# Rotary embedding on one core: the two early rows of batch 0 in one transfer or in two

## The chip, the cores and the metric

The kernel runs on one core of a Trainium2 chip. The metric is the device time of one execution in microseconds (us), the median of several runs. A profile is one further execution, recorded instruction by instruction and, for the DMA engines, packet by packet. VectorE does the arithmetic, ScalarE converts types, GpSimd and SyncE issue the transfers, and 16 DMA engines carry them out. TensorE is not used.

## The reference

```python
batch, seq_len, num_heads, head_dim = (8, 2048, 16, 64)      # x is float32
x1, x2 = x[..., :32], x[..., 32:]
cos, sin = cos[None, :, None, :], sin[None, :, None, :]      # each (2048, 32)
out1 = x1 * cos - x2 * sin
out2 = x1 * sin + x2 * cos
return np.concatenate([out1, out2], axis=-1).astype(np.float32)
```

Every element of x is read once and every element of the output written once, 67.1 MB each way. The tables are the same for all batches and heads.

## The kernel before, in words

Each batch is laid over 128 partitions: partition p holds the J = 16 consecutive sequence positions 16p to 16p+15, which the texts call rows. A row has 16 heads of 64 elements, that is 1,024 elements. So one batch is a tile of 128 partitions by 16 rows by 1,024 elements. In memory a row of one partition is 4 KB of float32, a whole partition's part of a batch 64 KB.

The tile `buf` (f16) has room for five batches, and batch b lies in place b mod 5. The transfers that GpSimd issues convert on the way: a load reads float32 and writes f16 (`load`, line 71), a store reads f16 and writes float32 (`store`, line 81). All of these are tied by hand into one order, the ring (`in_ring`), which is also the order in which GpSimd issues them. They go through one queue, q0 in the profile. A load into a place that is in use waits until the store from there is done.

`rotate(b, j0, j1)` does the arithmetic on rows j0 to j1 of batch b with three VectorE operations: the swapped halves times sin into `v` (line 92), the batch times cos in place (line 98), and the sum in place (line 100). The minus sign is in the sin table, which ScalarE prepares (lines 104 and 105) as it narrows cos (line 106).

Batch 0 is treated apart, so that VectorE can begin before its big load is in. Its first two rows (JA = 2) are not loaded by GpSimd but by SyncE, as float32, into the tile `head` (line 42, queue q1, behind the sin table on the same queue). ScalarE narrows them into `buf` (line 107), VectorE rotates them, and GpSimd stores row 0 alone. The other fourteen rows come with `load(0)`. The issue order after the tables is: `load(0)`, `load(1)`; rotate rows 0 and 1 of batch 0; store row 0; load batches 2 and 3 together, and 4; rotate rows 2 to 15; store rows 1 to 15; then batch 1, batch 2 and so on. At the end the last two rows of batch 7 go out through `head` and SyncE (lines 134 and 135) behind the part of the store that the code calls `gate`.

Of the kernel before, what the change touches and what calls it, by code (L numbers as in the profile page):

```python
# [1 line left out]

# [4 lines left out]


@with_exitstack  # L10
def kernel(
    ctx: ExitStack,
    tc: tile.TileContext,
    x: bass.AP,
    cos: bass.AP,
    sin: bass.AP,
    out: bass.AP,
):
    nc = tc.nc
    f16 = mybir.dt.float16  # L20
    f32 = mybir.dt.float32

    B, S, H, D = x.shape
    Dh = D // 2
    P = nc.NUM_PARTITIONS
    J = S // P
    NBUF = 5

    const_pool = ctx.enter_context(tc.tile_pool(name="rope_const", bufs=1))
    io_pool = ctx.enter_context(tc.tile_pool(name="rope_io", bufs=1))  # L30
    tmp_pool = ctx.enter_context(tc.tile_pool(name="rope_tmp", bufs=1))

    JA = 2
    head = const_pool.tile([P, JA, H, D], f32)
    x0 = x[0].rearrange("(p j) h d -> p j (h d)", j=J)
    sin_f = const_pool.tile([P, J, Dh], f32)
    cos_f = const_pool.tile([P, J, Dh], f32)
    cos_h = const_pool.tile([P, J, Dh], f16)
    sin_h = const_pool.tile([P, J, D], f16)
    nc.scalar.dma_start(out=cos_f, in_=cos.rearrange("(p j) d -> p j d", j=J))  # L40
    nc.sync.dma_start(out=sin_f, in_=sin.rearrange("(p j) d -> p j d", j=J))
    nc.sync.dma_start(
        out=head.rearrange("p j h d -> p (j h d)"),
        in_=x0[:, 0:JA, :].rearrange("p j f -> p (j f)"),
    )

    buf = io_pool.tile([P, NBUF, J, H, D], f16)

    ring = []

    def in_ring(dma):
        if ring:
            tc.add_manual_dep(
                dma.ins,
                ring[-1].ins.name,
                mybir.DependencyInfo(mybir.DependencyClass.NoSync, mybir.DependencyReason.DATA),
                reason="order of the ring",
            )
        ring.append(dma)
        return dma  # L60

    def load(b, n=1):
        k = b % NBUF
        if n == 1:
            j0 = JA if b == 0 else 0
            dst = buf[:, k, j0:J, :, :].rearrange("p j h d -> p (j h d)")
            src = x[b].rearrange("(p j) h d -> p j (h d)", j=J)[:, j0:J, :].rearrange("p j f -> p (j f)")
        else:
            dst = buf[:, k : k + n, :, :, :].rearrange("p b j h d -> p b (j h d)")
            src = x[b : b + n].rearrange("b (p j) h d -> p b (j h d)", j=J)  # L70
        in_ring(nc.gpsimd.dma_start(out=dst, in_=src))  # L71

    def store(b, n=1, j0=0, j1=J):
        k = b % NBUF
        if n == 1:
            src = buf[:, k, j0:j1, :, :].rearrange("p j h d -> p (j h d)")
            dst = out[b].rearrange("(p j) h d -> p j (h d)", j=J)[:, j0:j1, :].rearrange("p j f -> p (j f)")
        else:
            src = buf[:, k : k + n, :, :, :].rearrange("p b j h d -> p b (j h d)")
            dst = out[b : b + n].rearrange("b (p j) h d -> p b (j h d)", j=J)  # L80
        return in_ring(nc.gpsimd.dma_start(out=dst, in_=src))  # L81

    def rotate(b, j0=0, j1=J):
        v = tmp_pool.tile([P, J, H, D], f16)
        n = j1 - j0
        js = slice(j0, j1)
        xt = buf[:, b % NBUF, js, :, :]
        shape = [P, n, H, 2, Dh]
        sin_b = sin_h[:, js, :].rearrange("p j (e d) -> p j e d", e=2).unsqueeze(2).to_broadcast(shape)
        cos_b = cos_h[:, js, :].unsqueeze(2).to_broadcast([P, n, 2 * H, Dh])  # L90
        xe = xt.rearrange("p j h (e d) -> p j h e d", e=2)
        nc.vector.tensor_mul(  # L92
            out=v[:, js, :, :].rearrange("p j h (e d) -> p j h e d", e=2),
            in0=xe[:, :, :, ::-1, :],
            in1=sin_b,
        )
        xw = xt.rearrange("p j h (e d) -> p j (h e) d", d=Dh)
        nc.vector.tensor_mul(out=xw, in0=xw, in1=cos_b)  # L98
        xa = xt.rearrange("p j h d -> p (j h d)")
        nc.vector.tensor_add(out=xa, in0=xa, in1=v[:, js, :, :].rearrange("p j h d -> p (j h d)"))  # L100

    load(0)
    load(1)
    nc.scalar.copy(out=sin_h[:, :, Dh:D], in_=sin_f)  # L104
    nc.scalar.mul(out=sin_h[:, :, 0:Dh], in_=sin_f, mul=-1.0)  # L105
    nc.scalar.copy(out=cos_h, in_=cos_f)  # L106
    nc.scalar.copy(  # L107
        out=buf[:, 0, 0:JA, :, :].rearrange("p j h d -> p (j h d)"),
        in_=head.rearrange("p j h d -> p (j h d)"),
    )  # L110
    rotate(0, 0, JA)
    store(0, 1, 0, 1)
    load(2, 2)
    load(4)
    rotate(0, JA, J)
    store(0, 1, 1, J)
    rotate(1)
    store(1)
    rotate(2)
    store(2)  # L120
    load(5, 2)
    load(7)
    rotate(3)
    rotate(4)
    store(3, 2)
    rotate(5)
    rotate(6)
    store(5, 2)
    rotate(7)
    gate = store(7, 1, 0, 9)  # L130
    store(7, 1, 9, J - JA)
    last = buf[:, 7 % NBUF, J - JA : J, :, :].rearrange("p j h d -> p (j h d)")
    dst = out[B - 1].rearrange("(p j) h d -> p j (h d)", j=J)[:, J - JA : J, :].rearrange("p j f -> p (j f)")
    nc.scalar.copy(out=head.rearrange("p j h d -> p (j h d)"), in_=last)  # L134
    end = nc.sync.dma_start(out=dst, in_=head.rearrange("p j h d -> p (j h d)"))
    tc.add_manual_dep(
        end.ins,
        gate.ins.name,
        mybir.DependencyInfo(mybir.DependencyClass.Sync, mybir.DependencyReason.DATA),
        reason="the last rows go out behind this part",  # L140
    )


# [1 line left out]
_INS = ['x', 'cos', 'sin']  # L145
_OUTS = [((8, 2048, 16, 64), 'float32')]


# [23 lines left out]
```

## Time and profile before

| what | us |
| --- | --- |
| median of three runs (316.48 to 316.59) | 316.5 |
| the profiled execution | 316.39 |
| its span, first to last instruction | 314.6 |
| VectorE busy | 209.1 |
| GpSimd busy | 8.6 |
| ScalarE busy | 6.7 |
| wait of VectorE for batch 2 to be loaded, from 72.99 us | 10.1 |
| wait of VectorE for batch 5 to be loaded, from 161.66 us | 36.1 |

The span is what the profile covers; the device time has some 1.8 us around it. The DMA queues carried 2,528 packets (99.09 MB, 98.1% of the engines' time) on GpSimd's q0, 432 packets (2.36 MB) on SyncE's q1 and 144 (0.26 MB) on ScalarE's q10. These megabytes count what was written; HBM was read for 67.63 MB and written for 67.11 MB. Of one transfer, each of the 16 engines carries the packets of eight partitions, one packet per partition, and then a 4-byte packet that closes it.

In the views, a line like "23.87 7.63 DVE L92 ..." of the timeline gives the start, the duration, the engine and the line of the kernel; what stands in brackets is how long the engine sat idle before and what released it. "POOL" is GpSimd, "SP" SyncE, "ACT" ScalarE and "DVE" VectorE, and a "q" behind a name is that engine's own queue of commands.

### The profile page before, as it was taken

The numbers are of one execution on the slowest core, as the hardware profiler recorded it, in microseconds if no ns is written. First come the engines' busy times: TensorE is split into PE (matmuls) and PEld (weight loads), VectorE is DVE, ScalarE is ACT, GpSimd is POOL, SyncE is SP. The second block draws the span as 40 slices with busy tenths as digits, with TensorE's granted clock in tenths as the row PEclk, the third lists the DMA queues.
The fourth block names the chain that finished last, engine by engine and source line by source line (L and its number), as shares of the span: only waits on it lengthen the run. The fifth ranks groups of instructions, "written<-read, shape, count | busy, mean of one in ns | idle before, by whom it ended". The sixth has DMA issues, their size and how long they took to land.

```text
span 314.6 us, 114 instructions
## 1 busy us (share of the span) xinstructions
DVE 209.1 (66%) x27; ACT 6.7 (2%) x6; POOL 8.6 (3%) x18
## 2 busy tenths in 40 slices
DVE  0039999992499999999950000899999999910000
ACT  3200000000000000000000000000000000020000
POOL 1020000000000000000010000000000000010000
DMA  7999999999999899999999999999999999999998
GB/s 240 252 242 200 200 267 200 200 267 200 200 200 325 375 500 400 400 400 533 400 200 221 246 200 200 246 221 333 400 508 425 400 400 525 408 400 400 433 425 342
DMA packets 3104, 101.71 MB, mean 323 GB/s; under 512 B 288, under 2 KB 288, under 8 KB 672
## 3 DMA queue, kind: packets, MB, share of 16 engines
q0 software_dynamic: 2528, 99.09, 98.1%
q1 hardware_dynamic: 432, 2.36, 1.9%
q10 hardware_dynamic: 144, 0.26, 0.2%
HBM read 67.63 MB, written 67.11 MB: 428 GB/s over the span
## 4 chain that ended last, share of the span: by engine, by line
DVE 65%; another core or an unknown queue 15%; DMA 7%; ACT 1%; issue 0%; DVEq 0%; ACTq 0%; PEldq 0%
DVE buf L98 22%; DVE v L92 22%; DVE buf L100 22%; DMA buf<-in_x_dram 7%; ACT head L134 1%; DVEq L92 0%; ACTq L134 0%; PEldq L167 0%
## 5 line engine op out<-in xcount | busy, mean ns | idle before, releaser
L92 DVE TENSOR_TENSOR v<-buf,sin_h 128x16384 f16<-128x16384 f16 (+2 forms) x9 | 69.7, 7744 | 66.6 <-DMA buf<-in_x_dram 51.3
L98 DVE TENSOR_TENSOR buf<-buf,cos_h 128x16384 f16<-128x16384 f16 (+2 forms) x9 | 69.7, 7744 | 0.3
L100 DVE TENSOR_TENSOR buf<-buf,v 128x16384 f16<-128x16384 f16 (+2 forms) x9 | 69.7, 7744 | 0.3
L81 POOL DMA_DIRECT2D out_dram<-buf x8 | 4.7, 584 | 219.2 <-DVE buf L100 219.2
L134 ACT CAST head<-buf 128x2048 f32<-128x2048 f16 x1 | 1.9, 1897 | 261.3 <-DVE buf L100 261.3
L71 POOL DMA_DIRECT2D buf<-in_x_dram x6 | 3.7, 628 | 49.7 <-DMA out_dram<-buf 48.9
L107 ACT CAST buf<-head 128x2048 f16<-128x2048 f32 x1 | 1.9, 1897 | 7.1 <-DMA head<-in_x_dram 7.1
L104 ACT ACT_TABLE_LOAD x1 | 1.3, 1283 | 1.2 <-PEq L156 1.2
L104 ACT CAST sin_h<-sin_f 128x512 f16<-128x512 f32 x1 | 0.6, 617 | 2.0 <-DMA sin_f<-in_sin_dram 2.0
L105 ACT ACTIVATE sin_h<-sin_f 128x512 f16<-128x512 f32 x1 | 0.6, 624 | 0.0
L106 ACT CAST cos_h<-cos_f 128x512 f16<-128x512 f32 x1 | 0.6, 601 | 0.0
L156 POOL MEMSET const-float32-0.0<- 128x1 f32 x1 | 0.1, 98 | 0.2 <-issue 0.2
L156 POOL MEMSET const-bfloat16-1.0<- 128x1 bf16 x1 | 0.1, 101 | 0.0
L156 POOL MEMSET const-uint8-127<- 128x1 uint8 x1 | 0.1, 99 | 0.0
L156 POOL MEMSET const-float32-1.0<- 128x1 f32 x1 | 0.1, 98 | 0.0
## 6 DMA issues: line engine op xcount, KB each, us to landing
buf<-in_x_dram POOLq DMA_DIRECT2D x2, 8192.0 KB, 60.3
buf<-in_x_dram POOLq DMA_DIRECT2D x3, 4096.0 KB, 57.4
out_dram<-buf POOLq DMA_DIRECT2D x1, 7680.0 KB, 73.5
out_dram<-buf POOLq DMA_DIRECT2D x1, 4608.0 KB, 28.6
buf<-in_x_dram POOLq DMA_DIRECT2D x1, 3584.0 KB, 22.5
out_dram<-buf POOLq DMA_DIRECT2D x1, 2560.0 KB, 34.1
head<-in_x_dram SPq DMA_DIRECT2D x1, 1024.0 KB, 12.0
out_dram<-head SPq DMA_DIRECT2D x1, 1024.0 KB, 8.4
```

The source lines that it names most:

```text
L71: in_ring(nc.gpsimd.dma_start(out=dst, in_=src))
L81: return in_ring(nc.gpsimd.dma_start(out=dst, in_=src))
L92: nc.vector.tensor_mul(out=v[:, js, :, :].rearrange("p j h (e d) -> p j h e d", e=2), in0=xe[:, :, :, ::-1, :], in1=sin_b,)
L98: nc.vector.tensor_mul(out=xw, in0=xw, in1=cos_b)
L100: nc.vector.tensor_add(out=xa, in0=xa, in1=v[:, js, :, :].rearrange("p j h d -> p (j h d)"))
L104: nc.scalar.copy(out=sin_h[:, :, Dh:D], in_=sin_f)
L105: nc.scalar.mul(out=sin_h[:, :, 0:Dh], in_=sin_f, mul=-1.0)
L106: nc.scalar.copy(out=cos_h, in_=cos_f)
L107: nc.scalar.copy(out=buf[:, 0, 0:JA, :, :].rearrange("p j h d -> p (j h d)"), in_=head.rearrange("p j h d -> p (j h d)"),)
L134: nc.scalar.copy(out=head.rearrange("p j h d -> p (j h d)"), in_=last)
L156: nc = _bacc.Bacc("TRN2", target_bir_lowering=False, num_devices=1)
```

## The change

SyncE asks for the two rows of `head` in two transfers, of one row each, 4 KB per partition instead of 8. Narrowing is a small function of one row, `narrow(j)`. Row 0 is narrowed and rotated early and stored as before; row 1 is narrowed after the loads of batches 2 to 4 are written down in the program, and is rotated together with rows 2 to 15. The stores, the loads and their order stay as they are, and so does the end of the kernel.

```diff
-    nc.sync.dma_start(
-        out=head.rearrange("p j h d -> p (j h d)"),
-        in_=x0[:, 0:JA, :].rearrange("p j f -> p (j f)"),
-    )
+    for j in range(JA):
+        nc.sync.dma_start(out=head[:, j, :, :].rearrange("p h d -> p (h d)"), in_=x0[:, j, :])
...
+    def narrow(j):
+        nc.scalar.copy(
+            out=buf[:, 0, j, :, :].rearrange("p h d -> p (h d)"),
+            in_=head[:, j, :, :].rearrange("p h d -> p (h d)"),
+        )
...
-    nc.scalar.copy(
-        out=buf[:, 0, 0:JA, :, :].rearrange("p j h d -> p (j h d)"),
-        in_=head.rearrange("p j h d -> p (j h d)"),
-    )
-    rotate(0, 0, JA)
+    narrow(0)
+    rotate(0, 0, 1)
     store(0, 1, 0, 1)
     load(2, 2)
     load(4)
-    rotate(0, JA, J)
+    narrow(1)
+    rotate(0, 1, J)
     store(0, 1, 1, J)
```

## Prediction

> **What bounds the kernel now.** I read the page first, its second part before its fourth, because the two disagree. The rows of slices (40 slices of 7.9 us each):
>
> ```profile
> DVE  0039999992499999999950000899999999910000
> ...
> DMA  7999999999999899999999999999999999999998
> ...
> DVE 65%; another core or an unknown queue 15%; DMA 7%; ACT 1%; issue 0%; DVEq 0%; ACTq 0%; PEldq 0%
> ```
>
> The chain gives 65% to VectorE, but VectorE has stretches of zeros and the DMA engines have none. To decide between them I cut the span at the borders of the transfer stages (busy time by stretch; the last two columns are the DMA share, 1.00 for all 16 engines busy, and GB/s written):
>
> ```profile
> 0.00:4.00 4.00, 0.00 (x0) 1.28 (x1) 1.41 (x6) 1.00 0.53 169
> 4.00:24.00 20.00, 3.80 (x4) 3.55 (x4) 1.80 (x3) 1.00 1.08 255
> 24.00:45.00 21.00, 20.93 (x3) 0.00 (x0) 0.00 (x0) 1.00 1.01 225
> 45.00:102.00 57.00, 46.67 (x7) 0.00 (x0) 1.08 (x2) 1.00 1.01 226
> 102.00:159.00 57.00, 56.80 (x7) 0.00 (x0) 1.24 (x2) 1.00 1.02 427
> 159.00:217.00 58.00, 21.75 (x4) 0.00 (x0) 1.27 (x2) 1.00 1.01 226
> ```
>
> From 4 us on the share is 1.00 or more, whatever VectorE does: 56.80 of 57 us in one stretch, 21.75 of 58 in another. (Loads show half the GB/s because they write 2 bytes for 4 read; above 1.00, because packet records overlap by some 0.02 us.) I added up from the packet records how many of the 16 engines had a packet open at each moment: they lose 1.86 us before 2 us of the span, 0.24 us from 2 to 4, 0.21 us after 312, and nothing worth counting between. The span is therefore the time that 16 busy engines need for a fixed set of packets, and the chain's 65% is work beside them. The start, where the change lies:
>
> ```profile
> 1.17 0.43 SPq L42 DMA_DIRECT2D head<-in_x_dram  x1
> 1.24 1.21 POOL L71 DMA_DIRECT2D buf<-in_x_dram  x2 [0.80 <-PEq L167]
> ...
> 5.51 0.60 ACT L106 CAST cos_h<-cos_f 128x512 f16<-128x512 f32 x1
> 13.22 1.90 ACT L107 CAST buf<-head 128x2048 f16<-128x2048 f32 x1 [7.11 <-DMA head<-in_x_dram]
> 15.15 1.23 DVE L92 TENSOR_TENSOR v<-buf,sin_h 128x2048 f16<-128x2048 f16 x1 [15.15 <-ACT buf L107]
> ...
> 19.19 0.54 POOL L81 DMA_DIRECT2D out_dram<-buf  x1 [16.74 <-DVE buf L100]
> 19.72 1.27 POOL L71 DMA_DIRECT2D buf<-in_x_dram  x2
> 23.87 7.63 DVE L92 TENSOR_TENSOR v<-buf,sin_h 128x14336 f16<-128x14336 f16 x1 [4.98 <-DMA buf<-in_x_dram]
> ```
>
> The head's 8 KB packets (eight per engine, 0.309 us each) run alone from 3.65 us. At 5.49 us the GpSimd queue q0 gets its first packet, 2.13 us long, and from there each engine takes one packet of q0 and one of SyncE's q1 in turn. Most engines have passed six head packets by then; the other two and the closing 4-byte packet each wait for one of q0's, so the head is in at 12.93 and ScalarE starts 0.29 us later.
>
> **The change part by part.**
>
> *The split transfer.* Per engine, eight 8 KB packets and one closing packet become sixteen of 4 KB and two closing ones. A 4 KB packet on q1 isn't in the trace. Its neighbours there are 2 KB at one packet each 0.080 us and 8 KB at one each 0.306 us; the straight line gives 0.155 us, so 16 × 0.155 = 2.48 us for 8 × 0.306 = 2.45: +0.03 us. One closing packet more: +0.01 to 0.02 us. A q1 packet that alternates with q0's shows 0.322 us for 0.309, and some three more will alternate: 3 × 0.013 = +0.04 us. At the end SyncE waits for one more semaphore, 0.06 us a step in its row of waits, partly behind the last landing: 0 to 0.06 us. Ends: as lower end 0 (the same bytes; a gain from a fuller start could not exceed the 0.24 us lost from 2 to 4 us), as upper end the 4096-byte packets of the early store, at least 0.172 us each, so 16 × 0.172 − 2.45 = +0.30 us. I take the line, because it joins rows of the same queue and direction: +0.1 us in all.
>
> *Is the second transfer there in time?* SyncE's first issue at 0.74 has its first packet at 1.74, 1.00 us later; the head's issue at 1.17 is followed by packets at 3.65, directly behind the sin table's. The second row's issue would run from about 1.6 to 2.0 us. Row 0 takes 8 × 0.155 = 1.24 us, from 3.65 or 3.88 by engine, up to 4.9 or 5.13. ScalarE's cos transfer, issued in the same moment as sin's, has its first packet 0.77 us behind sin's; as spacing between two transfers this puts row 1's packets at 3.65 + 0.77 = 4.42 at the latest, 0.5 us before they are needed. Late, they would leave engines idle until q0's 5.49 us: at most 0.6 us. I take 0.
>
> *Row 0, early.* It lands at about 5.2, seen at 5.4 us, but ScalarE is at L106 until 6.11. The narrowing of 1,024 elements lies between 0.617 us (512) and 1.897 (2,048): 1.04 us, done at 7.1. Three VectorE operations of 1,024 elements: by the rows of 2,048 (1.225) and 14,336 (7.626) 0.521 us per thousand, so 0.69 each, done near 9.3. The store and the loads of batches 2 to 4 are issued from about 9.5 instead of 19.19. That is worth nothing: q0 runs in ring order, and the packets of that store, issued at 19.19 in the kernel before, started at 42.59, behind loads 0 and 1. An issue ten microseconds earlier only waits ten longer.
>
> *Row 1, later.* Three or four of its packets pass before 5.49; the four or five left and the closing one go in rounds of 2.3 us behind q0's, so it lands near 17 to 19.5 us. Its narrowing takes 1.04 us and is done by 20.9 at the latest, before load 0 releases VectorE (23.87). Cover: 3 us. If all of it went in rounds, the rotation would begin about 1 us late.
>
> *The longer rest.* Fifteen rows: 7.626 + 0.533 = 8.16 us for each of three operations, 3 × 0.533 = +1.60 us, ending near 48.5 instead of 46.83. Queued behind it on VectorE are batch 1 and on GpSimd the stores of batches 0 and 1. Batch 1 ends at 74.6 instead of 72.99; VectorE then idles until 83.06 for batch 2 in any case, which hides the 1.6 us with 8.5 to spare. The two stores move to 48.8 and 74.9; their packets start at 101.8 and 119.9, behind the loads, 45 us or more of cover. Nothing of this reaches the DMA engines.
>
> Sum against the profiled execution: 316.39 us (span 314.6, 1.8 around it) + 0.1 = 316.5. Its time is 0.11 under the median of the runs, 316.5, so the forecast on the median is 316.6.
>
> **A rule that speaks against the change.** The Trainium skill, page "DMA: Bandwidth & Descriptors", section "Anatomy of one DMA — SWDGE (gpsimd) path", fits a fixed 2.0 us to each transfer, and its section "Rules for kernel authors" asks for 1 MiB or more per DMA. If that fixed part were not overlapped (and held for SyncE's queue), the second transfer would cost an estimated 2.0 us and the time be 318.5. By that rule no gap of such size should be missing between sin's last packet and the head's first, and the trace shows none: 3.56 and 3.65 us. What it would be as a mechanism of this kernel, priced from rows, is the first rival.
>
> **The rivals.**
>
> *Slower: a start-up per transfer that the engines sit through.* In the trace 669 to 971 ns stand on some of the sin table's early packets instead of 84; the same on row 1's first packet would hold each engine 0.6 to 0.9 us, and a full issue-to-packet time 1.0 us. All of it would come out at the end, since no DMA engine has slack: 317.2 to 317.6. For it: the trace has no second new transfer on a busy SyncE queue but the head. Against: the head's own first packets show 309 ns, like its others. It decides from 0.6 us idle per engine. 7%.
>
> *Slower: the chain is right, and VectorE's time counts.* Then +1.6 us pass through: 318.1. Against: the 10 us wait ahead of batch 2, and a DMA share of 1.00 through it. 3%.
>
> *Faster: the earlier issue fills the queue.* Needs a moment in which q0 ran dry behind load 1; the records have none. A gain of at most the 2.1 us lost before 4 us: 314.5 to 316. 3%.
>
> *The early narrowing waits for both rows after all* (the change doesn't split the wait): row 0 would be stored from about 23 us, still 20 us ahead of its turn at 42.6: 316.6 again. It goes with the forecast, 2%.
>
> **How the numbers follow.** No change, 85% and the 2% beside it, gives 316.6. Its ends are 316.3 (the 0.24 us gained) and 317.1 (upper packet cost 0.3 and part of the 0.6 idle); that leaves out about 15%, and the range needn't reach the rivals. A measurement tells about 0.2%, 0.63 us, from no change. Slower by more: both slower rivals, 10%; faster: 3%; within: 87%.
>
> **What the profile after would show.** Right: DMA share near 1.00 in every stretch after 4 us; `buf<-head` twice at about 1.04 us, the first at 6.1, the second at 17 to 20; the rotation of 128x15360 at 23.9 with three times 8.16; batch 2's rotation still at 83.2. Wrong: a dip of the share at 4.9 to 5.5 us; batch 2 later than 83.8, which would mean that the DMA engines themselves lost time; or row 1 narrowed later than 23 us, which would mean that the packets do not take turns as I read them.

## The result, and the profile after

The changed kernel takes 317.29 us (median of 10 runs, 316.92 to 317.91) where the kernel before takes 316.49 (10 runs, 316.29 to 316.87): a ratio of 1.0025, 95% interval 1.0017 to 1.0033. It is slower by 0.8 us. The profiled execution took 317.57 us, with a span of 315.8.

The page of the changed kernel, slices and chain:

```profile
DVE  0107999997399999999960000799999999910000
...
DMA  9999999999999899999999999999999999999897
...
DVE 66%; another core or an unknown queue 14%; DMA 7%; ACT 1%; issue 0%; SPq 0%; DVEq 0%; ACTq 0%
```

VectorE still has its stretches of zeros, and the DMA engines still have none. The last slices of the DMA row, 897 instead of 998, hint at something. The start of the changed kernel's timeline:

```profile
1.15 0.90 SPq L43 DMA_DIRECT2D head<-in_x_dram  x2
...
5.15 0.60 ACT L110 CAST cos_h<-cos_f 128x512 f16<-128x512 f32 x1
6.22 1.04 ACT L82 CAST buf<-head 128x1024 f16<-128x1024 f32 x1 [0.47 <-DMA head<-in_x_dram]
...
9.74 0.54 POOL L79 DMA_DIRECT2D out_dram<-buf  x1 [7.29 <-DVE buf L104]
...
24.87 1.04 ACT L82 CAST buf<-head 128x1024 f16<-128x1024 f32 x1 [17.60 <-DMA head<-in_x_dram]
25.95 8.16 DVE L96 TENSOR_TENSOR v<-buf,sin_h 128x15360 f16<-128x15360 f16 x1 [16.50 <-ACT buf L82]
...
84.34 8.69 DVE L96 TENSOR_TENSOR v<-buf,sin_h 128x16384 f16<-128x16384 f16 x1 [7.67 <-DMA buf<-in_x_dram]
```

Row 0 is narrowed and stored when the prediction said. Row 1 comes much later, at 24.87 us, and the long rotation begins 2.1 us behind that of the kernel before. The wait ahead of batch 2 takes that up: VectorE still idles 7.67 us there. But batch 2 itself begins 1.2 us later, released by a load. In the kernel before it was

```profile
83.16 8.69 DVE L92 TENSOR_TENSOR v<-buf,sin_h 128x16384 f16<-128x16384 f16 x1 [10.16 <-DMA buf<-in_x_dram]
```

The prediction had named a batch 2 later than 83.8 us as the sign that the DMA engines themselves have lost time.

Where they lost it is seen at the end. The windows of the last two microseconds, first the kernel before, then the changed one (the last two columns are the DMA share and GB/s):

```profile
312.50:313.00 0.50, 0.00 (x0) 0.00 (x0) 0.00 (x0) 1.00 0.97 410
313.00:313.50 0.50, 0.00 (x0) 0.00 (x0) 0.00 (x0) 1.00 0.13 49
313.50:314.00 0.50, 0.00 (x0) 0.00 (x0) 0.00 (x0) 1.00 0.00 0
```

```profile
312.50:313.00 0.50, 0.00 (x0) 0.00 (x0) 0.00 (x0) 1.00 0.93 393
313.00:313.50 0.50, 0.00 (x0) 0.00 (x0) 0.00 (x0) 1.00 0.78 328
313.50:314.00 0.50, 0.00 (x0) 0.00 (x0) 0.00 (x0) 1.00 0.16 66
314.00:314.60 0.60, 0.00 (x0) 0.00 (x0) 0.00 (x0) 1.00 0.03 14
```

Before, the share falls from full to nothing within half a microsecond. After, it fades over more than one, and a share of 0.03 over 0.6 us is 0.3 us of one engine out of sixteen. The kernel waits for the slowest engine: SyncE's last wait for a transfer ends 0.36 us behind the last closing packet, at 313.77 us before and at 314.95 after.

The packet records date this. The 16 packets that close load 0, one per engine, lie between 23.02 and 23.46 us before, between 23.32 and 24.32 after. From the close of load 1 on, at 43 us, the 16 closing packets of every later transfer lie as far apart as there, 0.32 us before and 1.23 after, so that nothing evens the engines out: they finish from 313.09 to 313.41 us before, from 313.36 to 314.59 after. The fastest engine is 0.27 us later, the slowest 1.18. Of that 1.18, 0.86 stand at the close of load 0; the rest comes up to the close of load 1, where 16 of 144 packets that begin near 40 us are slow in both kernels (up to 2.72 us before and 2.86 after, for 2.43). More on these below. And the lag begins with row 0's own packets. Alone on their queue, 4 KB packets take 0.159 us. Of the 128 packets of row 0, 22 take longer, up to 0.789 us; all of them begin between 3.8 and 4.7 us. Row 0 closes on the engines from 4.89 to 5.90 us, a spread of one microsecond, right where the queue of loads takes over.

### The profile page after: what moved, and what is told of

Its sections match the earlier page's. It is cut to its first block, busy times and chain, and to the rows that moved or that the text cites. A ratio compares the mean times of both kernels' runs of the same rounds, so it can differ in the third digit from the quotient of the medians.

```text
span 315.8 us, 118 instructions
## 1 busy us (share of the span) xinstructions
DVE 209.1 (66%) x27; ACT 6.9 (2%) x7; POOL 8.6 (3%) x18
## 4 chain that ended last, share of the span: by engine, by line
DVE 66%; another core or an unknown queue 14%; DMA 7%; ACT 1%; issue 0%; SPq 0%; DVEq 0%; ACTq 0%
DVE v L96 22%; DVE buf L102 22%; DVE buf L104 22%; DMA head<-in_x_dram 7%; ACT head L136 1%; ACT buf L82 0%; SPq L43 0%; SPq L41 0%; DVEq L96 0%; ACTq L136 0%
## 5 line engine op out<-in xcount | busy, mean ns | idle before, releaser
L82 ACT CAST buf<-head 128x1024 f16<-128x1024 f32 x2 | 2.1, 1044 | 18.1 <-DMA head<-in_x_dram 18.1
```

The costliest lines, as they stand in the source:

```text
L82: nc.scalar.copy(out=buf[:, 0, j, :, :].rearrange("p h d -> p (h d)"), in_=head[:, j, :, :].rearrange("p h d -> p (h d)"),)
```

## The experiments

Theory: the slowest engine sets the end, and row 0's transfer makes the engines uneven. The rivals: VectorE's later rotation counts; or nine more packets per engine cost all engines alike. What makes row 0's packets slow was open at first; two theories on it fell and a third stood. In the table, "slow" counts the head's packets before 6 us that take more than 0.175 us (4 KB) or 0.325 (8 KB); "load 0 closes" and "engines end" give the first and the last engine in the one profiled execution. The ratios stand against the kernel before on the same chip; a median is of 9 to 11 executions, for `two_halves` of 6.

| kernel | median us | ratio, 95% interval | slow | load 0 closes | engines end |
| --- | --- | --- | --- | --- | --- |
| before | 316.49 | | 0 | 23.02 to 23.46 | 313.09 to 313.41 |
| changed | 317.29 | 1.0025 (1.0017 to 1.0033) | 22 | 23.32 to 24.32 | 313.36 to 314.59 |
| after_again | 317.25 | 1.0023 (1.0013 to 1.0033) | 18 | 23.31 to 24.04 | 313.47 to 314.24 |
| split_only | 317.33 | 1.0024 (1.0016 to 1.0033) | 19 | 23.20 to 24.15 | 313.55 to 314.49 |
| late_only | 316.67 | 1.0001 (0.9992 to 1.0010) | 1 | 23.07 to 23.55 | 313.28 to 313.79 |
| small_packets | 316.45 | 0.9997 (0.9988 to 1.0006) | 0 | 23.09 to 23.51 | 313.12 to 313.52 |
| dummy_second | 316.54 | 1.0000 (0.9991 to 1.0009) | 0 | 22.97 to 23.38 | 313.24 to 313.65 |
| two_halves | 317.47 | 1.0031 (1.0019 to 1.0043) | 47 | 23.89 to 24.39 | 313.74 to 314.24 |
| row1_waits | 317.25 | 1.0023 (1.0014 to 1.0032) | 23 | 22.90 to 23.91 | 313.26 to 313.95 |
| row1_act | 317.06 | 1.0020 (1.0011 to 1.0029) | 8 | 23.14 to 23.82 | 313.16 to 314.12 |
| row0_only | 317.14 | 1.0019 (1.0010 to 1.0028) | 15 | 23.26 to 23.88 | 313.34 to 314.04 |
| pitch_16k | 317.28 | 1.0024 (1.0015 to 1.0033) | 40 | 23.58 to 24.41 | 313.52 to 314.25 |
| pitch_4k | 316.69 | 1.0002 (0.9993 to 1.0010) | 0 | 23.41 to 23.93 | 313.25 to 313.77 |
| head_first | 316.86 | 1.0009 (1.0000 to 1.0017) | 24 | 22.96 to 23.51 | 313.23 to 313.87 |

One reading goes through all fourteen: the profiled time less the last engine's end is 2.97 to 3.02 us every time (316.39 − 313.41 = 2.98, 317.57 − 314.59 = 2.98). The last engine is the time.

**The changed kernel again.**

> The changed kernel once more. Theory (spread): every DMA engine has its own fixed packets, and the slowest engine sets the end. Then the 16 closing packets of load 0 lie about 1 us apart again (0.44 us in the kernel before), and the profiled time is above 316.4 us by about as much as the last engine's end is above 313.4. Rival (VectorE): the rotation that begins at 25.95 instead of 23.87 us costs the time; then it is 317.3 whatever the spread. Rival (packets): nine more packets per engine cost all engines alike; then the fastest engine is as late as the slowest.

Slow packets again, 18 for 22. Load 0 closes over 0.73 us and not 1 us as expected, and the engines end over 0.76 us (313.47 to 314.24) where the first profile had 1.23. The last end is 0.83 us above that of the kernel before, the profiled time 0.84 (317.23 for 316.39). How far the last engine falls back differs between executions, and the profiled time follows it.

**The two halves of the change.** `split_only` keeps the arithmetic of the kernel before and only splits the transfer; `late_only` keeps the one transfer and only changes the arithmetic.

```diff
# split_only, against the kernel before
-    nc.sync.dma_start(out=head.rearrange("p j h d -> p (j h d)"), in_=x0[:, 0:JA, :].rearrange("p j f -> p (j f)"))
+    for j in range(JA):
+        nc.sync.dma_start(out=head[:, j, :, :].rearrange("p h d -> p (h d)"), in_=x0[:, j, :])
# late_only, against the changed kernel: the same lines the other way round
```

> The two transfers alone, with the arithmetic of the kernel before (both rows narrowed and rotated early, fourteen later). Spread and packets: as the changed kernel, 317.1 to 317.5 us. VectorE: the rest of batch 0 is 14 rows again, but it now waits for row 1, which lands with load 0; with the early rotation behind that the rest ends later than in either kernel, so at least 317.3.

> The arithmetic of the changed kernel alone (row 0 early, row 1 with the other fourteen), the head in one transfer. Spread and packets: 316.5 us, as the kernel before. VectorE: between 316.5 and 317.3, by how much of the lateness is the longer rest (1.6 us of it).

All of it lies in the transfer: 1.0024 for the split alone, 1.0001 for the arithmetic alone. In `late_only` the longer rest is there and nothing follows:

```profile
23.98 8.16 DVE L98 TENSOR_TENSOR v<-buf,sin_h 128x15360 f16<-128x15360 f16 x1 [5.33 <-DMA buf<-in_x_dram]
...
83.54 8.69 DVE L98 TENSOR_TENSOR v<-buf,sin_h 128x16384 f16<-128x16384 f16 x1 [8.83 <-DMA buf<-in_x_dram]
```

Batch 2 still waits 8.83 us for its load. So the longer rest costs nothing. That its later beginning costs nothing either is seen in `row1_waits` below.

**Small packets in one transfer.** Rows 0 and 1 lie 32 bytes apart in the tile, so that one transfer brings them in two packets of 4 KB per partition.

```diff
-    head = const_pool.tile([P, JA, H, D], f32)
+    head_rows = const_pool.tile([P, JA, H * D + 8], f32)
...
+    nc.sync.dma_start(out=head_rows[:, :, 0 : H * D], in_=x0[:, 0:JA, :])
```

> The kernel before with the head in one transfer, but of 4 KB packets (its two rows lie 32 bytes apart in the tile), so one closing packet per engine instead of two. If small packets at the front of SyncE's queue make the engines uneven: 317.0 to 317.4 us, and a spread of some 1 us at the end of load 0. If it is the second transfer (its commands written while the first one runs): 316.5 and a spread below 0.5. Packets: 316.6 to 316.8 without more spread.

None of the 178 packets of 4 KB before 6 us is slow, and the time is 316.45. So neither the size nor the number of the packets costs anything here. That left the second transfer as such, and I took it that writing its commands disturbs the first.

**A second transfer of next to no bytes.**

```diff
+    spare = const_pool.tile([P, 8], f32)
+    nc.sync.dma_start(out=spare, in_=x0[:, 0, 0:8])
```

> The kernel before, and behind the head's one transfer a second one on SyncE that moves 32 bytes per partition into a tile nobody reads (4 KB in all, eight packets per engine of next to no time). Theory (commands): what slows the head's packets at 3.8 to 4.7 us, unevenly by engine, is that the commands of a further transfer are being written then; it needs no bytes. Then 8 KB packets near 4 us show more than 0.309 us, the closing packets of load 0 spread by 0.7 us or more, and the time is 316.9 to 317.4 us. Rival (splitting the bytes): 316.5 to 316.7, no slow packets.

This theory fell: not one slow packet, ratio 1.0000. A further transfer of next to no bytes on SyncE costs nothing that can be measured.

**Two transfers by partitions.**

```diff
+    for p0 in (0, P // 2):
+        nc.sync.dma_start(
+            out=head[p0 : p0 + P // 2].rearrange("p j h d -> p (j h d)"),
+            in_=x0[p0 : p0 + P // 2, 0:JA, :].rearrange("p j f -> p (j f)"),
+        )
```

> The kernel before with the head in two transfers by partitions (0 to 63, 64 to 127), so that all packets keep 8 KB and their number, and only a closing packet per engine is added. Theory (commands): slow packets near 4 us and 316.9 to 317.4 us. Rival (a small packet or a half row per transfer is what is slow): 316.5 us.

Just above the expected time, and with another signature: 47 of 63 packets of 8 KB are slow, up to 0.656 us, 0.80 us per engine on average. The first engine, too, ends 0.65 us later than before, and the engines end only 0.5 us apart. This looks like a second effect, of 64 partitions at a time; it stays open. For the question at hand the run is inconclusive.

**Row 1 later, or on another queue.** `row1_waits` lets SyncE ask for row 1 when row 0 is in; `row1_act` lets ScalarE ask for it.

```diff
# row1_waits
+    tc.add_manual_dep(row1.ins, row0.ins.name, mybir.DependencyInfo(mybir.DependencyClass.Sync, ...), ...)
# row1_act
+    nc.scalar.dma_start(out=head[:, 1, :, :].rearrange("p h d -> p (h d)"), in_=x0[:, 1, :])
```

> The changed kernel, but SyncE asks for row 1 only when row 0 is in (about 5.2 us). Theory (commands): the packets of row 0 show no more than 0.16 us each and row 0 closes on all engines within 0.5 us; against that stands idle time between row 0's close (about 4.9) and the first packet of load 0 (4.9 to 5.5 us), so 316.5 to 317.1 us. If the slow packets stay, they belong to row 0's own small transfer, and it is 317.3 or more.

> The changed kernel with row 1 asked for by ScalarE, behind cos, on its own queue. Theory (commands): they are written at much the same time, so slow packets near 4 us again and 317.0 to 317.4 us. Rival (two transfers in a row on one queue are what is slow): 316.5 to 316.7 us.

With row 1 asked for at 6.15 us, when row 0 has closed on all engines (4.94 to 5.82 us), row 0 still has 23 slow packets and the time is still 317.25: the slow packets belong to row 0's own transfer. The run also answers the rival of VectorE. Row 1 lands so late that the rotation begins 4.2 us behind that of the changed kernel, and the time is the same:

```profile
30.17 8.16 DVE L102 TENSOR_TENSOR v<-buf,sin_h 128x15360 f16<-128x15360 f16 x1 [20.66 <-ACT buf L88]
...
83.70 8.69 DVE L102 TENSOR_TENSOR v<-buf,sin_h 128x16384 f16<-128x16384 f16 x1 [2.82 <-DMA buf<-in_x_dram]
```

With both rows under way together there are fewer slow packets, 8, the slowest 0.338 us, 0.04 us per engine on average. The end is uneven all the same, and 317.06 us is more than these packets explain; that stays open.

**Row 0 alone, and read from elsewhere.** What is left of row 0's transfer is what it reads: 4 KB out of every 64 KB, on 16 engines at once. `row0_only` asks for row 0 alone (row 1 comes with load 0). `pitch_4k` and `pitch_16k` are the changed kernel in every instruction and packet, except that the first transfer reads 128 rows that lie 4 or 16 KB apart; row 0 of batch 0 then holds other positions' data.

```diff
# row0_only, against the changed kernel
+    nc.sync.dma_start(out=head[:, 0, :, :].rearrange("p h d -> p (h d)"), in_=x0[:, 0, :])
-            j0 = JA if b == 0 else 0
+            j0 = 1 if b == 0 else 0
-    narrow(1)
# pitch_4k (s = 1) and pitch_16k (s = 4)
+    near = x[0, 0 : s * P].rearrange("(p s) h d -> p s (h d)", s=s)
+    nc.sync.dma_start(out=head[:, 0, :, :].rearrange("p h d -> p (h d)"), in_=near[:, 0, :])
```

> The changed kernel without the second transfer: SyncE asks for row 0 alone, row 1 comes with load 0 (fifteen rows). Theory (pitch): a transfer that reads 4 KB out of every 64 KB, all 16 engines in step, is itself slow and uneven; so slow packets near 4 us as in the changed kernel, row 0 closing over 0.8 to 1 us, and 316.9 to 317.3 us. Rival (it takes a second transfer of bytes beside it): no slow packets and 316.4 to 316.7 us.

> The changed kernel, but the first transfer reads 128 rows that lie one behind the other (pitch 4 KB instead of 64); so row 0 of batch 0 comes from other positions, all else is unchanged. Theory (pitch): no slow packets near 4 us, load 0 closes within 0.5 us on all engines, 316.5 to 316.8 us. Rival (any transfer of one 4 KB packet per partition does it, or what follows later in the changed kernel, such as the early issue of loads 2 to 4): 317.1 to 317.4 us.

> The same with a pitch of 16 KB. Theory (pitch): between the two, 316.6 to 317.2 us. Rival: 317.1 to 317.4 us.

`row0_only` has no second transfer and no more packets than the kernel before (3,104 in both), and is still slower by 0.62 us, with 15 slow packets. `pitch_16k` has 40 and is at 317.28. `pitch_4k` has none, its engines stay together, and it is at 316.69. Its VectorE is nearly as late as the changed kernel's (25.54 us for 25.95):

```profile
24.46 1.04 ACT L83 CAST buf<-head 128x1024 f16<-128x1024 f32 x1 [17.19 <-DMA head<-in_x_dram]
25.54 8.16 DVE L97 TENSOR_TENSOR v<-buf,sin_h 128x15360 f16<-128x15360 f16 x1 [16.09 <-ACT buf L83]
```

The ends of the DMA engines, `row0_only` first, then `pitch_4k`, then `pitch_16k`:

```profile
313.00:313.50 0.50, 0.00 (x0) 0.00 (x0) 0.00 (x0) 1.00 0.70 295
313.50:314.00 0.50, 0.00 (x0) 0.00 (x0) 0.00 (x0) 1.00 0.16 66
```

```profile
313.00:313.50 0.50, 0.00 (x0) 0.00 (x0) 0.00 (x0) 1.00 0.71 295
313.50:314.00 0.50, 0.00 (x0) 0.00 (x0) 0.00 (x0) 1.00 0.01 0
```

```profile
313.00:313.50 0.50, 0.00 (x0) 0.00 (x0) 0.00 (x0) 1.00 0.93 393
313.50:314.00 0.50, 0.00 (x0) 0.00 (x0) 0.00 (x0) 1.00 0.25 98
```

`row0_only` and `pitch_4k` are both full to 313.3 or so; the one then has stragglers, a share of 0.16 over half a microsecond, the other has none. The expectation of the theory for `pitch_16k`, something between the two, was wrong: 16 KB is as bad as 64.

These ends hold a second difference, though. The slow packets of load 1 near 40 us are there in the profiles of ten of the fourteen kernels, the kernel before among them: 15 or 16 of 144, up to 2.98 us for 2.43, 0.14 to 0.38 us per engine on average. `row1_waits` has 11 (0.08 us), `pitch_16k` 4 (0.03 us), `pitch_4k` and `two_halves` none. Why is not known. When load 0 closes, the last engine of `pitch_4k` is no earlier than that of `row0_only` (23.93 and 23.88 us); the 0.27 us between their ends come up only behind that. The clean pair is `pitch_16k` and `pitch_4k`, the same instructions and packets and hardly a slow packet near 40 us: 24.41 and 23.93 us at the close of load 0, 314.25 and 313.77 at the end, medians of 317.28 and 316.69. At 64 KB it is shown that row 0 by a transfer of its own costs time: `row0_only` takes 1.0019 of the time of the kernel before and `late_only` 1.0001, and both have the slow packets near 40 us. How much of the 0.6 us between the changed kernel and `pitch_4k` is the pitch is less sure, since 0.2 to 0.3 us may belong to those.

**The head first.** One more order, in search of a faster kernel: the head ahead of the tables.

```diff
-    nc.sync.dma_start(out=sin_f, in_=sin.rearrange("(p j) d -> p j d", j=J))
+    nc.scalar.dma_start(out=sin_f, in_=sin.rearrange("(p j) d -> p j d", j=J))
```

> The kernel before with the head's one transfer first on SyncE's queue, and sin ahead of cos on ScalarE's. The same bytes and packets in another order; if the engines' common work sets the time, 316.4 to 316.7 us. If the wait of the first packets near 2 us (0.4 to 0.7 us per engine in all runs so far) can be hidden behind others, 316.0 to 316.3 us.

Now it is the head's packets that are slow near 2 us, as the sin table's are in the others; the wait moves and isn't hidden. At 316.86 us, ratio 1.0009, it is no gain, and outside both ranges that were expected. (That wait was put at 0.4 to 0.7 us per engine in all runs; counted over 84 ns a packet, it is 0.1 us in `row1_act` and 0.3 to 0.8 in the others that have it.) No kernel here beats both the kernel before and the noise.

## Why the prediction was wrong, point by point

**What bounds the kernel** was named rightly, the DMA engines, and then read too coarsely. "The time that 16 busy engines need for a fixed set of packets" treats the sixteen as one. Each has packets of its own, the spread of 1.23 us at 43 us is still 1.23 at the end, and so the end is that of the slowest. A mean DMA share of 1.00 cannot show an engine that is a microsecond behind the others; the fading share at the very end can.

**The split transfer** is the step that failed: +0.1 us in the sum, +0.8 measured, beyond the upper end of 317.1. The straight line from 2 KB to 8 KB gave 0.155 us a packet, and 0.159 is what most of them take; `pitch_4k`, with all the extra packets and rounds, is 0.17 us above its kernel before. (It lacks the slow packets near 40 us, which cost the kernel before 0.19 us per engine, so the packets' own share may be up to some 0.4 us, an estimate.) So the term was about right for the packets and left out what they read. The neighbouring rows were no neighbours in that: the sin table is read without gaps, the head of the kernel before 8 KB out of every 64. What the term left out goes with the reads of 4 KB out of every 64: slow packets that cost 0.04 to 0.19 us per engine on average in the runs that have them at that pitch, and up to 0.63 us in a single packet (0.789 for 0.159). The records don't name a packet's engine, so how much of this falls on the last one isn't shown.

**Is the second transfer there in time?** Yes; no engine runs dry: counted as the prediction counts, less than 0.01 us is lost from 4.5 to 6 us. **The rule that speaks against the change**: `dummy_second` adds a transfer and no time (316.54 for 316.48), so nothing near 2.0 us was paid.

**Row 0, early** held: narrowed at 6.22 us, 1.04 us long, stored at 9.74, and worth nothing.

**Row 1, later** held in kind and not in size: it was narrowed at 24.87 us, past the 23 that the prediction named as a sign of being wrong. The first packets of load 0 came at each engine's close of row 0, from 4.89 us, and not at 5.49; all nine packets of row 1 then took turns, and it landed with load 0. The rotation was 2.1 us late where the worst case in the text had about 1. `row1_waits`, later still, shows that this cost nothing. **The longer rest**, 8.16 us for each operation, was exact and hidden as said.

**The rivals.** The first, a start-up that the engines sit through, had the right size (317.2 to 317.6, at 7%), but by luck, since the reason is another: the slow packets are row 0's, not those of the second transfer, and a second transfer of next to no bytes is free. (Its price was read from early packets of the sin table; the shortest of these slow ones took 632 ns, not 669.) VectorE's rival and the faster one fell. The chance of 87% for no change rested on prices for a packet by its size alone.

What stays open: why reads at 16 and 64 KB apart are slow when 4 KB is taken and not when 8 KB is, or when both rows come in one transfer. The Trainium skill, page "DMA: Bandwidth & Descriptors", section "Latency and other measured facts", tells of transfers that slow down when the rows of the partitions lie large powers of two apart, from 2 MiB on, and at 512 KiB nearly at full rate; it supposes that streams in step meet in the same part of the memory. The pitches here, 16 and 64 KB, are smaller than any in that row, and every run that reads row 0 by a transfer of its own at one of them has slow packets; whether it is the same thing, no run shows. Row 1's packets in the changed kernel have the same pitch and, taking turns with load 0, show 0.172 us in 122 of 128 cases (0.27 at most) from 7.0 to 24.2 us, as do all 128 of `pitch_4k`; so the engines may have to read in step for it, which wasn't tried by itself. Open, too, are the slow packets of load 1 near 40 us.

## What to carry to other kernels

When the DMA engines are busy throughout, ask for the slowest one, not for their mean share: look at how the share fades at the end, and at the spread of the packets that close a transfer. In all fourteen kernels the spread of the engines at 43 us was still there at the end, so lateness on one engine is not made up by the others. A transfer that is split along a row reads fewer bytes at the same distance: price it by a row with the same distance, and if there is none, leave the range wide.

## What was not expected of the hardware

- 4 KB reads at 64 KB or 16 KB from partition to partition: 15 to 23 of 128 packets slow at 64 KB when a row is read alone, 40 at 16 KB, up to 0.789 us for 0.159; none at 4 KB, and none of 178 where both rows come in one transfer.
- A transfer for 64 partitions: 47 of 63 packets of 8 KB slow, 0.80 us per engine on average, in one run.
- The last packets of load 1, near 40 us: 15 or 16 of 144 slow in ten of fourteen kernels, up to 2.98 us for 2.43, and none in two.
- GpSimd's queue took its first turn on every engine right behind the closing packet of row 0 (4.89 to 5.91 us) in the changed kernel, but only after six packets of 8 KB (5.49 us) in the kernel before.
